# An encoder block on one core: the second blocks of its experts made small and interleaved, and its weight splits moved ahead

## The chip, the cores and the metric

The kernel runs on one core of a Trainium2 chip. The metric is the device time of one execution in microseconds (us), less is better. Engines are named as in the profile: PE is TensorE (matrix products), DVE is VectorE, ACT is ScalarE, POOL is GpSimd, and SP issues DMAs.

## The reference

The input is 2048 tokens of width 1024 in float32. The block normalises them, projects them, mixes them by windowed attention and by a bidirectional mLSTM, projects back and adds the residual. Then it sends each token to two of 32 experts:

```python
x = x + u @ w_out[l]
x = x + hier_moe(rmsnorm(x, norm2_g[l]), ...)        # top-1 group, then top-2 experts in it
...
return (jax.nn.silu(xb @ w_gate[e]) * (xb @ w_up[e])) @ w_down[e]     # 1024 -> 512 -> 1024
...
y = jnp.zeros((T, D), ys.dtype).at[row_tok].add(ys * row_w[:, None].astype(ys.dtype))
```

The routing of the reference's inputs gives 15 of the 32 experts more than 128 rows (130 to 180): experts 1, 7, 8, 10, 11, 14 to 17, 19, 20 and 27 to 30. None has more than 192.

## The kernel before

The first two thirds (projections, attention, mLSTM, merge, routing) are the same in both kernels. The change is in the last stage, the experts, which are run one after the other from 0 to 31.

Products are taken in split precision. A float32 matrix is written as a big half, rounded to the product's format, and a small half, the rest; a product is then three matrix products: big by big, small by big, big by small. For weights this is done on chip. An expert's weights come as six loads of 1 MB (`raw`, `rawd`; the SP queue issues them) and are cut into 12 pieces of 128x1024, eight of gate and up (`j` 0 to 7), four of down (8 to 11). `split` makes a piece: ACT copies the big half (`ehi`, L1560), and POOL for the pieces 1, 5, 8 and 10 (`POOL_J`), DVE for the others, subtracts the small half (`elo`, L1562). `wsplit(n)` splits piece n of all experts in a row (expert e begins at 12 e), and when both pieces of a load are split it issues the load six further on.

```python
    def wsplit(n):
        ...
        wts[n] = split(raws[n // 2], n % NPC)
        if n % 2:
            del raws[n // 2]
            wload(n // 2 + NRAW)
```

A block is up to 128 rows of an expert. POOL gathers its rows (`xg`; `xgB` for the second block) by an indirect DMA, PE transposes them (`xturn`, L1589), ACT and DVE split them into `xhi` and `xlo`. Then `Block.head` takes 48 products of 512 columns for gate and up (two halves `h` of the expert's width by eight row blocks by three), `act` makes `ha` (ACT's silu L1627, DVE's multiplication L1628), `turn` transposes it (PE L1634) and splits it (ACT L1635, DVE L1636), and 24 products follow for down, the last 12 in `Block.tail`. ACT and DVE scale half of the result each (`y`, L1703 and L1704), and POOL adds it to the output by an indirect DMA, a scatter (L1705). So a block is 72 products of 512 columns.

Each engine works through its own queue in the order of the program; semaphores order the queues against each other. The order is written by hand (`manual_schedule`): `between(i)` is called at five places of `head`, and the table `SPLITS` says which pieces are split at which place. When an expert begins, pieces 0 and 1 are split; 2 to 7 are split at the start of `head`, the rest in it. A second block runs within `tc.If(v > 1)` after the first, with its own 72 products over the same split weights, and nothing is split beside it.

Of the kernel before, what the change touches and what calls it, by code (L numbers as in the profile page):

```python
# [20 lines left out]
P = 128  # L21
# [19 lines left out]
def bucket_table():  # L41
    """Relative position to bucket, as one-hot rows, and the window's mask as a last row."""
# [12 lines left out]
class Chains:  # L55
    """Queues of generators, each advanced a step at a time between blocks of matrix products."""
# [55 lines left out]
def _body(tc, nc, A, out, scr_ext, upto, es):  # L112
# [68 lines left out]
    # gates of the mLSTM, all tokens: [i|f] x tile x (dir, head)  # L181
# [19 lines left out]
    PW = 272  # L201

    class Stream:
# [9 lines left out]
        def dma(self, n):  # L213
            """load half n % 2 of piece n // 2"""
# [70 lines left out]
    # order of the column pieces in a chunk of tokens  # L285
# [30 lines left out]
    def run_mms(mms, nsub=6):  # L316
        """mms: list of (out, lhsT, rhs, start, stop); chains advance between sub-blocks."""
# [11 lines left out]
    # ================= first half: projections, attention, forward mLSTM =================  # L329
# [19 lines left out]
    def small_loads():  # L349
# [7 lines left out]
        # per-channel vectors: conv taps (5), conv bias, merge biases, all halved  # L357
# [6 lines left out]
    def setup():  # L364
        """attention bias [query, head, key], per-channel columns, empty slots"""
# [26 lines left out]
        # a row of zeros past the tokens, weight 0  # L392
# [21 lines left out]
    # ---- rms norm and transposition of a tile of x  # L414
# [33 lines left out]
    # ---- attention  # L448
# [197 lines left out]
    def mload(t, d):  # L646
        """a tile's q and v; forward its k, backward what the forward pass left: k by rows and k q"""
# [15 lines left out]
    def mhead(n, t, d):  # L663
        """what a tile of the recurrence does without the state, at most a tile ahead of it"""
# [48 lines left out]
    def mtile(n, t, d):  # L713
        """one tile of the recurrence"""
# [71 lines left out]
    def mpost(n, t, h_):  # L786
        """both directions joined, normed and gated"""
# [32 lines left out]
    # ---- convolution over time, silu  # L820
# [17 lines left out]
    def conv_tail():  # L838
        """the last two tokens, with zeros behind them"""
# [77 lines left out]
    def qkv_done(c):  # L917
        """forward tiles of the mLSTM once a chunk's q, k and v are there"""
# [27 lines left out]
    # ---- projections  # L946
# [115 lines left out]
    # ================= second half: backward mLSTM, merge, output projection, routing =================  # L1062
# [12 lines left out]
    # the first tiles of these kinds, for the order of the kinds in memory  # L1075
# [7 lines left out]
    def after(t):  # L1083
        """makes what fills a tile wait for the first gated products"""
        nc.gpsimd.tensor_copy(t, uhi[:, 0, 0:1].bitcast(F32))
# [47 lines left out]
    def yprep_first(c):  # L1133
        """the same for the first chunk, in memory that holds the products later"""
# [41 lines left out]
    def bank(c, u):  # L1176
        """where the routing of a tile keeps its products"""
# [3 lines left out]
    def norm2(c, u):  # L1181
        """the residual and its norm go out; router logits of the tile, short of the norm's factor"""
# [44 lines left out]
    def table():  # L1227
        """rows and weights of the first two blocks of every expert, from the chunks before the last"""
# [367 lines left out]
    class Block:  # L1596
# [41 lines left out]
        def down_hi(self, k, h):  # L1638
            if k == 0:
                if h == 0:  # L1640
                    self.dn = []
# [155 lines left out]
```

## Time and profile before

| what | value |
|---|---|
| time, median of 3 runs (lowest to highest) | 2780.01 us (2776.28 to 2781.15) |
| profiled execution, first to last instruction | 2774.9 us |
| PE busy, of that span | 2562.3 us (92%) |
| DVE, ACT, POOL busy | 1556.6, 1283.7, 1243.0 us |
| experts' stage, 1786.6 to 2763.7 | 977.1 us, PE busy 888.2 |

Only the span of the profiled execution is given; the median of the runs lies 5.1 us above it. That PE is busy for 92% does not tell that it works at its pace: products are pipelined, and the time of one in a row is longer than the distance from one to the next.

### The profile page before, as it was taken

To read this page: it belongs to the slowest core of one execution; us is meant where nothing else is said; L and a number is where in the kernel's file an instruction comes from. 1 tells how busy PE (TensorE), PEld (TensorE's weight loads), DVE (VectorE), ACT (ScalarE), POOL (GpSimd) and SP (SyncE) were. 2 spreads that over 40 slices of the span, in tenths; PEclk is the share of its full clock that TensorE was granted. 3 is DMA by queue.
4 is the path that set the end of the run, shared out by engine and by line. 5 is a ranking of instruction groups with operands and counts; after the bars stand their busy time and mean duration, and the time that the engine had idled before them with its cause. 6 is when DMAs were issued, how large, how long until landed. Compare 5 with 4: busy or idle time off the path is not lost. (4 is left out here: it accounts for less than half of the span.)

```text
span 2774.9 us, 39144 instructions
## 1 busy us (share of the span) xinstructions
PE 2562.3 (92%) x14112; PEld 2129.0 (77%) x14113; DVE 1556.6 (56%) x2537; ACT 1283.7 (46%) x2500; POOL 1243.0 (45%) x1029
## 2 busy tenths in 40 slices
PE   7999999999999999978998989799999999988997
PEld 6778977897789787757977878677777777766775
DVE  4454445454545645558594937667454544567544
ACT  4444545454445444433332422357553544556543
POOL 5444444244433442324444445357643543545433
PEclk9999999999999999989999999899999999999998
DMA  5534434453345345477765644679876876779763
GB/s 159 156 113 149 135 111 121 141 160 107 114 137 161 114 127 164 148 195 213 230 199 179 186 152 127 223 252 344 283 257 191 297 242 195 266 232 324 267 194 109
DMA packets 348967, 518.68 MB, mean 187 GB/s; under 512 B 24747, under 2 KB 212228, under 8 KB 348748
## 3 DMA queue, kind: packets, MB, share of 16 engines
q1 hardware_dynamic: 332140, 460.03, 50.9%
q0 software_dynamic: 15440, 51.60, 7.9%
q10 hardware_dynamic: 1168, 4.21, 0.4%
q8 instruction: 126, 2.06, 0.3%
q14 instruction: 93, 0.76, 0.1%
HBM read 420.30 MB, written 95.47 MB: 186 GB/s over the span
## 5 line engine op out<-in xcount | busy, mean ns | idle before, releaser
L239 POOL TENSOR_TENSOR wlo<-wraw,whi 128x512 fp32r<-128x512 f32 (+1 forms) x422 | 572.7, 1386 | 472.4 <-ACT whi L236 454.4
L1618 PE MATMUL mm<-elo,xhi 128*128 128x512 f32 x752 | 276.2, 419 | 87.1 <-DVE elo L1562 50.5
L1562 DVE TENSOR_TENSOR elo<-raw,ehi 128x1024 fp32r<-128x1024 f32 x192 | 297.2, 1589 | 39.8 <-ACT ehi L1560 36.0
L1615 PE MATMUL mm<-ehi,xhi 128*128 128x512 f32 x752 | 307.6, 409 | 0.0
L319 PE MATMUL mm<-hThi,whi 128*128 128x512 f32 x768 | 306.9, 400 | 0.0
L319 PE MATMUL mm<-hTlo,whi 128*128 128x512 f32 x768 | 304.4, 396 | 0.0
L319 PE MATMUL mm<-hThi,wlo 128*128 128x512 f32 x768 | 304.0, 396 | 0.0
L1615 PE MATMUL mm<-ehi,xlo 128*128 128x512 f32 x752 | 302.4, 402 | 1.3 <-issue 1.3
L236 ACT ACTIVATE whi<-wraw 128x512 fp32r<-128x512 f32 (+1 forms) x424 | 233.4, 622 | 136.9 <-PE mm L319 59.1
L319 PE MATMUL mm<-whi,hThi 128*128 128x256 f32 (+1 forms) x896 | 260.3, 291 | 3.9 <-ACT ev L898 1.8
L319 PE MATMUL mm<-wlo,hThi 128*128 128x256 f32 (+1 forms) x896 | 256.0, 286 | 1.1 <-POOL wlo L239 1.1
L319 PE MATMUL mm<-whi,hTlo 128*128 128x256 f32 (+1 forms) x896 | 255.8, 285 | 0.0
L1618 PEld LDWEIGHTS mm<-elo,xhi 128*128 128x128 f32 x752 | 146.9, 198 | 139.8 <-DVE elo L1562 64.3
L1560 ACT ACTIVATE ehi<-raw 128x1024 fp32r<-128x1024 f32 x256 | 253.0, 1048 | 1.7 <-issue 0.5
L1705 POOL DMA_INDIRECT out<-y,idx x47 | 102.3, 2176 | 263.4 <-ACT ehi L1560 237.9
L1562 POOL TENSOR_TENSOR elo<-raw,ehi 128x1024 fp32r<-128x1024 f32 x64 | 156.4, 2444 | 127.9 <-ACT ehi L1560 127.2
L1562 POOL TENSOR_TENSOR elo<-rawd,ehi 128x1024 fp32r<-128x1024 f32 x64 | 163.9, 2560 | 79.0 <-ACT ehi L1560 79.0
L319 PEld LDWEIGHTS mm<-whi,hThi 128*128 128x128 f32 x896 | 170.2, 190 | 7.9 <-ACT ev L898 2.1
L319 PEld LDWEIGHTS mm<-wlo,hThi 128*128 128x128 f32 x896 | 170.3, 190 | 3.6 <-issue 1.6
L1615 PEld LDWEIGHTS mm<-ehi,xlo 128*128 128x128 f32 x752 | 147.5, 196 | 30.5 <-DVE xlo L1591 0.4
L319 PEld LDWEIGHTS mm<-hThi,wlo 128*128 128x128 f32 x768 | 144.3, 188 | 34.0 <-issue 3.2
L319 PEld LDWEIGHTS mm<-whi,hTlo 128*128 128x128 f32 x896 | 170.0, 190 | 0.3 <-DVE hTlo L444 0.2
(421 smaller groups left out, 5872.6 us busy)
## 6 DMA issues: line engine op xcount, KB each, us to landing
wraw<-w_in SPq DMA_DIRECT2D x152, 512.0 KB
raw<-w_expert_gate SPq DMA_DIRECT2D x128, 512.0 KB
raw<-w_expert_up SPq DMA_DIRECT2D x128, 512.0 KB
rawd<-w_expert_down SPq DMA_DIRECT2D x64, 1024.0 KB
mg_s<-evg SPq DMA_DIRECT2D x64, 256.0 KB
gt<-mg_s SPq DMA_DIRECT2D x32, 512.0 KB
wraw<-w_out SPq DMA_DIRECT2D x32, 512.0 KB
xt<-x SPq DMA_DIRECT2D x16, 512.0 KB
```

The lines of the kernel that those rows point to most:

```text
L236: nc.scalar.activation(hi[:, ks, :W], r[:, k:k + 2, :W], AF.Copy)
L239: eng.tensor_sub(lo[:, ks, :W], r[:, k:k + 2, :W], hi[:, ks, :W].bitcast(F32))
L319: nc.tensor.matmul(o, l, r, start=st, stop=sp)
L1560: nc.scalar.activation(dst[0], src, AF.Copy)
L1562: eng.tensor_tensor(dst[1], src, dst[0].bitcast(F32), op=OP.subtract)
L1615: nc.tensor.matmul(self.gu[h], x_[:, k, :], self.wt(k)[0][:, h, :], start=k == 0 and i == 0, stop=False)
L1618: nc.tensor.matmul(self.gu[h], self.xs[0][:, k, :], self.wt(k)[1][:, h, :], start=False, stop=stop)
L1705: nc.gpsimd.indirect_dma_start(out=out, out_offset=bass.IndirectOffsetOnAxis(ap=self.idx, axis=0), in_=y, in_offset=None, compute_op=OP.add)
```

## The change

A second block now has at most 64 rows. Its rows' big and small halves stand side by side in the 128 columns of one operand, so that the product with a weight's big half and that with its small half give all four partial products, in two passes and not three: 32 products for gate and up, 16 for down (`Small`). The two sets of 64 result rows are added at the end: for gate and up by eight products with a stacked identity (`fold`), for down by ACT and DVE. Its gate and up products stand after `middle` of the first block, its folds and down products beside and behind the first block's last ones. An expert with more than 192 rows takes its further blocks in the loop at the end, one block at a time.

The splits are moved. Of the next expert, pieces 2, 3 and 4 are split within the first block (after its gate and up products); pieces 5 to 13 are split in one run after the expert's last product. (`nxt` is the next expert's first piece; 12 and 13 belong to the one after it.) At the start all 14 pieces that there is room for are split.

```diff
--- before.py
+++ after.py
...
+    nc.vector.tensor_scalar(nbf, cnt[0:1, :], 192.0, None, op0=OP.is_gt)
+    nc.vector.scalar_tensor_tensor(nbf, cnt[0:1, :], 127.0, nbf, op0=OP.add, op1=OP.mult)
...
+        def begin(self):
+            for k in range(0, 4, 2):
+                for h in range(2):
+                    self.up(h, k, k + 2)
+            self.up(0, 4, KT)
             self.act(0)
+            self.room()
+        def middle(self):
             self.up(1, 4, 7)
             self.turn(0)
+            self.up(1, 7, KT)
+        def after(self, between=lambda i: None):
             self.act(1)
+            between(0)
+            self.down(0, (0, 1))
+            self.down(1, (0, 1))
+            between(1)
+            self.room()
             self.turn(1)
+            between(2)
+        def end(self, between=lambda i: None):
             between(0)
+            self.down(0, (2, 3))
             between(1)
+            self.down(1, (2, 3))
+            between(2)
             y = self.y
             nc.scalar.activation(y[:, 0:512], self.dn[0], AF.Copy, scale=self.wgt)
             nc.vector.tensor_scalar(y[:, 512:], self.dn[1], self.wgt, None, op0=OP.mult)
             nc.gpsimd.indirect_dma_start(out=out, out_offset=bass.IndirectOffsetOnAxis(ap=self.idx, axis=0),
                                          in_=y, in_offset=None, compute_op=OP.add)
...
+    class Small:
...
+        def turn(self):
+            for k in range(KT):
+                nc.tensor.transpose(self.p[:, k, :], self.xg[0:64, k * P:(k + 1) * P], ident[0:64, 0:64])
+            nc.scalar.activation(self.xs[:, :, 0, :], self.p, AF.Copy)
+            nc.vector.tensor_sub(self.xs[:, :, 1, :], self.p, self.xs[:, :, 0, :].bitcast(F32))
+        def product(self, ps, lhs, w, h, n):
+            for k in range(n):
+                for m in range(2):
+                    nc.tensor.matmul(ps, lhs[:, k].rearrange("p a t -> p (a t)"), w(k)[m][:, h, :],
+                                     start=k == 0 and m == 0, stop=k == n - 1 and m == 1)
+        def up(self):
+            for h in range(2):
+                self.product(self.ps[h], self.xs, self.wt, h, KT)
+        def copy(self):
+            nc.scalar.activation(self.g[:, 0, :], self.ps[0], AF.Copy)
+            nc.vector.tensor_copy(self.g[:, 1, :], self.ps[1])
+        def fold(self, h):
+            p = self.p[:, 4 * h:4 * h + 4]
+            for k in range(4):
+                nc.tensor.matmul(p[:, k, :], self.g[:, h, k * P:(k + 1) * P], sel, start=True, stop=True)
+            a = self.a[:, h]
+            nc.scalar.activation(a, p[:, 0:2], AF.Silu)
+            nc.vector.tensor_mul(a, a, p[:, 2:4])
+            hs = self.hs[:, 2 * h:2 * h + 2]
+            nc.scalar.activation(hs[:, :, 0, :], a, AF.Copy)
+            nc.vector.tensor_sub(hs[:, :, 1, :], a, hs[:, :, 0, :].bitcast(F32))
+        def down(self):
+            y = self.g[0:64].rearrange("p h f -> p (h f)")
+            ps = self.ps
+            for h in range(2):
+                self.product(ps[h], self.hs, lambda k: self.wt(8 + k), h, 4)
+                cs = slice(512 * h, 512 * h + 512)
+                nc.scalar.activation(y[:, cs], ps[h][64:128, :], AF.Copy)
+                nc.vector.tensor_add(y[:, cs], ps[h][0:64, :], y[:, cs])
+            nc.gpsimd.tensor_scalar(y, y, self.wgt[0:64, :], None, op0=OP.mult)
+            nc.gpsimd.indirect_dma_start(out=out, out_offset=bass.IndirectOffsetOnAxis(ap=self.idx[0:64, :], axis=0),
+                                         in_=y, in_offset=None, compute_op=OP.add)
-    SPLITS = {0: (2, 3, 4, 5, 6, 7), 1: (8,), 2: (9, 10), 3: (11,), 4: (12,)}
...
-    for n in range(RING - NPC):
+    two = mo.tile([1, 32], I32, name="two")
+    twof = mo.tile([1, 2, 32], F32, name="twof")
+    for i, n in enumerate((float(P), float(P + 64))):
+        nc.vector.tensor_scalar(twof[:, i], cnt[0:1, :], n, None, op0=OP.is_gt)
+    nc.vector.tensor_sub(two, twof[:, 0], twof[:, 1])
+    sel = mo.tile([P, 64], F32, name="sel")
+    for o in (0, 64):
+        nc.vector.tensor_copy(sel[o:o + 64, :], ident[o:o + 64, o:o + 64])
+    for n in range(6):
         wsplit(n)
     xsA = xtiles("")
     for i in range(2):
         xturn(xg[0], xsA, i, "")
+    for n in range(6, RING):
+        wsplit(n)
     for e in range(N_EXP):
-        v = nc.values_load(nb[:, e:e + 1], min_val=0, max_val=S // P)
-        nxt = {}
+        v = nc.values_load(two[:, e:e + 1], min_val=0, max_val=1)
+        nxt = NPC * (e + 1)
+        w_e = lambda k, e=e: wts[NPC * e + k]
         xgB = mo.tile([P, D], F32, name="xgB")
-        with tc.If(v > 1):
-            nc.gpsimd.indirect_dma_start(out=xgB, out_offset=None, in_=h2_ap,
-                                         in_offset=bass.IndirectOffsetOnAxis(ap=idx[:, 32 + e:33 + e], axis=0))
+        with tc.If(v > 0):
+            nc.gpsimd.indirect_dma_start(out=xgB[0:64, :], out_offset=None, in_=h2_ap,
+                                         in_offset=bass.IndirectOffsetOnAxis(ap=idx[0:64, 32 + e:33 + e], axis=0))
+        if e + 2 < N_EXP:
+            xg[e + 2] = gather(idx[:, e + 2:e + 3], "")
+        A_ = Block(w_e, xsA, idx[:, e:e + 1], wgt[:, e:e + 1])
+        B_ = Small(w_e, xgB, idx[:, 32 + e:33 + e], wgt[:, 32 + e:33 + e])
+        A_.begin()
+        with tc.If(v > 0) as cmp:
+            B_.turn()
+            A_.middle()
+            B_.up()
+        with cmp.Else():
+            A_.middle()
         def between(i):
-            if i == 0 and e + 2 < N_EXP:
-                xg[e + 2] = gather(idx[:, e + 2:e + 3], "")
-            if i == 4 and held:
+            if i == 0:
+                wsplit(nxt + 2)
+                wsplit(nxt + 3)
+            if i == 1 and held:
                 put(*held.pop(0))
-            for j in SPLITS.get(i, ()):
-                wsplit(NPC * e + j)
-            if i == 4 and e + 1 < N_EXP:
-                nxt["x"] = xtiles("")
-                for h in range(2):
-                    xturn(xg[e + 1], nxt["x"], h, "")
-                wsplit(NPC * e + 13)
-        A_ = Block(lambda k: wts[NPC * e + k], xsA, idx[:, e:e + 1], wgt[:, e:e + 1], "")
-        A_.head(between)
-        xsA = nxt.get("x")
-        with tc.If(v > 1) as cmp:
-            xsB = xtiles("B")
-            A_.tail(lambda i: xturn(xgB, xsB, i, "B"))
-            B_ = Block(lambda k: wts[NPC * e + k], xsB, idx[:, 32 + e:33 + e], wgt[:, 32 + e:33 + e], "B", xgB)
-            B_.head()
-            B_.tail()
+            if i == 2:
+                wsplit(nxt + 4)
+                if e + 1 < N_EXP:
+                    xs = xtiles("")
+                    for h in range(2):
+                        xturn(xg[e + 1], xs, h, "")
+                    return xs
+        nx = {}
+        def after(i):
+            nx["x"] = between(i)
+        A_.after(after)
+        with tc.If(v > 0) as cmp:
+            B_.copy()
+            def beside(i):
+                if i in (1, 2):
+                    B_.fold(i - 1)
+            A_.end(beside)
+            B_.down()
         with cmp.Else():
-            A_.tail()
-    # further blocks of experts with many rows
+            A_.end()
+        xsA = nx.get("x")
+        for n in range(5, RING):
+            wsplit(nxt + n)
     v = nc.values_load(most, min_val=0, max_val=S // P)
-    with tc.If(v > 2):
+    with tc.If(v > 1):
         with tc.For_i(0, N_EXP, 1) as e:
             v = nc.values_load(nb[:, bass.ds(e, 1)], min_val=0, max_val=S // P)
-            with tc.For_i(2, v, 1) as i:
+            with tc.For_i(1, v, 1) as i:
...
```

Three places show how the queues change. POOL, from one expert's scatters to the next expert's gathers (`out<-y` and `out<-g` are scatters, `xgB` and `xg` the gathers, the `TENSOR_TENSOR` rows subtract small halves); before:

```order
L1705 DMA out<-y,idx 2176x1024
L1745 ISA
L1745 UNCONDITIONAL_BRANCH
L1722 TENSOR_LOAD nb
L1725 COMPARE_AND_BRANCH
L1726 DMA xgB<-h_s,idx 128x1024
L1725 UNCONDITIONAL_BRANCH
L1725 ISA
L1725 UNCONDITIONAL_BRANCH
L1576 DMA xg<-h_s,idx 128x1024
L1562 TENSOR_TENSOR elo<-raw,ehi 128x1024
L1562 TENSOR_TENSOR elo<-rawd,ehi 128x1024 x2
```

The same place in the changed kernel:

```order
L1679 DMA out<-y,idx 2176x1024
L1802 ISA
L1802 UNCONDITIONAL_BRANCH
L1564 TENSOR_TENSOR elo<-raw,ehi 128x1024
L1564 TENSOR_TENSOR elo<-rawd,ehi 128x1024 x2
L1564 TENSOR_TENSOR elo<-raw,ehi 128x1024
L1762 TENSOR_LOAD two
L1766 COMPARE_AND_BRANCH
L1767 DMA xgB<-h_s,idx 64x1024
```

The gathers stood ahead of POOL's subtractions for an expert and now stand behind four of them.

DVE, from one expert's `y` to the next expert's first `ha`; before:

```order
L1704 TENSOR_SCALAR y<-mm,wgt 128x512
L1745 UNCONDITIONAL_BRANCH
L1722 TENSOR_LOAD nb
L1725 COMPARE_AND_BRANCH
L1725 UNCONDITIONAL_BRANCH x2
L1562 TENSOR_TENSOR elo<-raw,ehi 128x1024 x5
L1628 TENSOR_TENSOR ha<-ha,mm 128x256
```

and in the changed kernel:

```order
L1678 TENSOR_SCALAR y<-mm,wgt 128x512
L1802 UNCONDITIONAL_BRANCH
L1564 TENSOR_TENSOR elo<-raw,ehi 128x1024 x2
L1564 TENSOR_TENSOR elo<-rawd,ehi 128x1024 x2
L1564 TENSOR_TENSOR elo<-raw,ehi 128x1024
L1762 TENSOR_LOAD two
L1766 COMPARE_AND_BRANCH
L1766 UNCONDITIONAL_BRANCH x2
L1623 TENSOR_TENSOR ha<-ha,mm 128x256
```

Five subtractions stand ahead of `ha` in both; the five were the running expert's pieces 2, 3, 4, 6 and 7, and are now 6, 7, 9, 11 and the next expert's 0.

PE, where the second block's rows are transposed. Before, behind the first block's last transposes, three quarters through it:

```order
L1589 MATMUL tr<-ident,xg 128x128 x8
L1745 COMPARE_AND_BRANCH
L1589 MATMUL tr<-ident,xgB 128x128 x4
L1644 MATMUL mm<-ehi,hh 128x512
L1645 MATMUL mm<-elo,hh 128x512
```

and now, behind the first 36 products of an expert, ahead of the other 12 of gate and up:

```order
L1617 MATMUL mm<-elo,xhi 128x512
L1775 COMPARE_AND_BRANCH
L1696 MATMUL tr<-ident,xgB 128x64 x8
L1617 MATMUL mm<-ehi,xhi 128x512
L1617 MATMUL mm<-ehi,xlo 128x512
L1617 MATMUL mm<-elo,xhi 128x512
```

PE's need of `xgB` has moved from the last quarter of the first block's products to their middle.

## Rows read from the trace of the kernel before

**Rows 1.** Stretches (experts 23, 24, 16, all): length, busy, clock, DMA share, GB/s.

```profile
2488.70:2512.60 23.90, 19.75 (x86) 15.40 (x85) 18.27 (x15) 14.69 (x20) 13.18 (x7) 0.93 0.91 310
2512.60:2532.90 20.30, 18.65 (x85) 14.54 (x84) 15.90 (x15) 14.79 (x20) 14.63 (x7) 1.00 0.93 315
2259.70:2298.20 38.50, 36.32 (x170) 29.05 (x169) 17.26 (x22) 18.10 (x27) 16.53 (x8) 1.00 0.67 218
1786.60:2763.70 977.10, 888.22 (x3941) 702.61 (x3940) 551.03 (x584) 520.56 (x711) 486.59 (x226) 0.96 0.76 251
```

**Rows 2.** PE's waits in the experts' stage: us in total, times, longest.

```profile
PE mm L1618 <- DVE elo L1562: 50.5, 20, 4.2
PE mm L1618 <- POOL elo L1562: 36.1, 19, 2.2
```

**Rows 3.** Timeline of PE in expert 23: start, us, instruction [idle before].

```profile
2494.33 0.39 PE L1615 MATMUL mm<-ehi,xlo 128*128 128x512 f32 x1
...
2495.92 0.39 PE L1618 MATMUL mm<-elo,xhi 128*128 128x512 f32 x1
2500.45 1.93 PE L1618 MATMUL mm<-elo,xhi 128*128 128x512 f32 x3 [4.15 <-DVE elo L1562]
2502.18 0.63 PE L1615 MATMUL mm<-ehi,xhi 128*128 128x512 f32 x1
...
2503.87 0.40 PE L1615 MATMUL mm<-ehi,xlo 128*128 128x512 f32 x1
```

**Rows 4.** Timeline of ACT at the start of expert 23.

```profile
2488.54 0.69 ACT L1703 ACTIVATE y<-mm,wgt 128x512 f32<-128x512 f32 x1 [0.82 <-ACT ehi L1560]
2489.14 5.80 ACT L1560 ACTIVATE ehi<-raw 128x1024 fp32r<-128x1024 f32 x6
```

**Rows 5.** Timeline of POOL in the same expert.

```profile
2490.45 2.46 POOL L1705 DMA_INDIRECT out<-y,idx  x1 [0.26 <-ACT ehi L1560]
...
2494.64 2.38 POOL L1562 TENSOR_TENSOR elo<-raw,ehi 128x1024 fp32r<-128x1024 f32 x1
2496.97 2.34 POOL L1562 TENSOR_TENSOR elo<-rawd,ehi 128x1024 fp32r<-128x1024 f32 x1
```

**Rows 6.** Timeline of DVE in the same expert.

```profile
2488.92 0.75 DVE L1704 TENSOR_SCALAR y<-mm,wgt 128x512 f32<-128x512 f32 x1 [0.81 <-issue]
2490.24 3.50 DVE L1562 TENSOR_TENSOR elo<-raw,ehi 128x1024 fp32r<-128x1024 f32 x3 [0.56 <-ACT ehi L1560]
2494.03 7.51 DVE L1562 TENSOR_TENSOR elo<-raw,ehi 128x1024 fp32r<-128x1024 f32 x2 [0.29 <-ACT ehi L1560]
```

**Rows 7.** Timelines of POOL and DVE in expert 4, the same place.

```profile
1899.55 2.47 POOL L1562 TENSOR_TENSOR elo<-raw,ehi 128x1024 fp32r<-128x1024 f32 x1
1901.99 3.39 POOL L1562 TENSOR_TENSOR elo<-rawd,ehi 128x1024 fp32r<-128x1024 f32 x1
...
1898.51 4.60 DVE L1562 TENSOR_TENSOR elo<-raw,ehi 128x1024 fp32r<-128x1024 f32 x2 [0.29 <-ACT ehi L1560]
```

**Rows 8.** The gathers by tile, xgB and then xg: from issue to landing.

```profile
DMA to landing us min/median/max: 8.2/8.4/9.8
...
DMA to landing us min/median/max: 5.3/8.4/10.2
```

**Rows 9.** Groups of the stage by form: busy us, mean ns, idle before.

```profile
L1628 DVE TENSOR_TENSOR ha<-ha,mm 128x256 f32<-128x256 f32 x94 | 39.6, 422 | 202.5 <-ACT ha L1627 202.5
L1590 ACT ACTIVATE xhi<-tr 128x512 fp32r<-128x512 f32 x94 | 52.5, 598 | 12.4 <-PE tr L1589 10.6
```

**Rows 10.** Timeline of PE: small products in routing, the first transposes, later ones.

```profile
1758.21 1.08 PE L1392 MATMUL mm<-fe,fh 128*128 128x64 f32 x8
...
1784.84 1.97 PE L1589 MATMUL tr<-ident,xg 128*128 128x128 f32 x8 [5.97 <-DMA xg<-h_s,idx]
...
2276.32 1.19 PE L1589 MATMUL tr<-ident,xg 128*128 128x128 f32 x8
2277.35 0.60 PE L1589 MATMUL tr<-ident,xgB 128*128 128x128 f32 x4
```

More of the change, by code (lines that the diff above doesn't have):

```diff
@@ L1604, in __init__ @@
                                   for i in range(2))
-            self.y = mo.tile([P, D], F32, name="y", tag="y" + tag)
-            self.gu = [self.ps(h) for h in range(2)]
-        def ps(self, h):
-            if self.tag:
-                return mp.tile([P, 512], F32, name="mm", tag=f"a{h}" + self.tag)
-            return mp.tile([P, 512], F32, name="mm", tag="a", bufs=3)
-        def up_x(self, h, k):
-            for i, x_ in enumerate(self.xs):
-                nc.tensor.matmul(self.gu[h], x_[:, k, :], self.wt(k)[0][:, h, :], start=k == 0 and i == 0, stop=False)
@@ L1617, in up_w, with ps @@
-        def up_w(self, h, k, stop=False):
-            nc.tensor.matmul(self.gu[h], self.xs[0][:, k, :], self.wt(k)[1][:, h, :], start=False, stop=stop)
+            self.y = mo.tile([P, D], F32, name="y")
+            self.gu = [self.ps() for h in range(2)]
+            self.dn = []
+        def ps(self):
+            return mp.tile([P, 512], F32, name="mm", tag="a", bufs=3)
         def up(self, h, k0, k1):
             for k in range(k0, k1):
-                self.up_x(h, k)
-                self.up_w(h, k, k == KT - 1)
+                hi, lo = self.wt(k)
+                for m, (x_, w_) in enumerate(((self.xs[0], hi), (self.xs[1], hi), (self.xs[0], lo))):
+                    nc.tensor.matmul(self.gu[h], x_[:, k, :], w_[:, h, :], start=k == 0 and m == 0,
+                                     stop=k == KT - 1 and m == 2)
@@ L1632, in turn @@
-            p = mp.tile([P, 4, P], F32, name="tr", tag="tr" + self.tag, bufs=1 if self.tag else 2)
+            a, hhi, hlo, p = self.a, self.hhi, self.hlo, self.p
             for k in range(2):
@@ L1672, in head @@
+        def begin(self):
[3 more added lines that the diff above has]
+            self.up(0, 4, KT)
             self.act(0)
-            between(2)
+            self.room()
+        def middle(self):
             self.up(1, 4, 7)
             self.turn(0)
-            self.up(1, 7, 8)
+            self.up(1, 7, KT)
+        def after(self, between=lambda i: None):
             self.act(1)
-            between(3)
-            for k in range(2):
-                self.down_hi(k, 0)
@@ L1681, in head @@
-            if self.tag:
-                for k in range(2):
-                    self.down_lo(k, 0)
-            for k in range(2):
-                self.down_hi(k, 1)
-            self.turn(1)
-            for h in range(1 if self.tag else 0, 2):
-                for k in range(2):
-                    self.down_lo(k, h)
-            between(4)
-        def tail(self, between=lambda i: None):
+            between(0)
+            self.down(0, (0, 1))
+            self.down(1, (0, 1))
+            between(1)
@@ L1772, in _body @@
                         wt[n] = split(r, n)
-                G = Block(wt.get, xs, ix, en[:, 1:2], "")
-                G.head()
-                G.tail()
+                G = Block(wt.get, xs, ix, en[:, 1:2])
+                G.begin()
+                G.middle()
+                G.after()
+                G.end()
 _INS = ["x", "norm1_g", "w_in", "attn_q_gain", "attn_k_gain", "attn_sink", "rel_bias_table",
```

70 lines of the change are left out of this document (24 added, 46 removed).

## The prediction

> **What bounds the kernel now.** Only the experts' stage differs between the two kernels, so I read it first, by stretch [rows 1]: 977.1 us of the 2774.9, PE busy for 888.2. An expert without a second block takes 20.3 us (24) or 23.9 (23), one with a second block 38.5 (16). Then PE's waits there [rows 2]: all but a few are for small halves of weights, 50.5 us for DVE's and 36.1 for POOL's. The timeline of PE shows one of them [rows 3]: products stand 0.227 us apart (seven steps from 2494.33 to 2495.92), then PE waits 4.15 us, and after it seven steps take 3.42 us (2500.45 to 2503.87) and not 1.6: the granted clock is at the lower of its two levels, 1.2 and not 2.4 GHz, which costs 1.8 more. The mean clock of that expert is 0.93; of the next, without so long a wait, 1.00 [rows 1].
>
> Why DVE is late stands in three timelines of expert 23, whose first product is at 2488.70; I call that moment T. ACT makes big halves 0.95 apart (six in 5.80) [rows 4]. POOL begins its scatter at T+1.75 and has 2.46 to do, then a gather, then two subtractions of 2.4 [rows 5]; the scatter needs DVE's half of `y`, which ends at T+1.0 [rows 6]. DVE subtracts in 1.17 (three in 3.50), but the pair at 2494.03 takes 7.51 [rows 6]: the first of it ends only when POOL's two are over (2499.31). In expert 4 a DVE subtraction that came during POOL's first got its turn behind it, and POOL's second took 3.39 for 2.34, waiting in turn [rows 7]. So POOL and DVE never subtract at the same time; mostly they alternate, and one of them can be passed over. The Trainium skill (SBUF — State Buffer, "Who interferes with whom") has it as a lock: a DVE instruction with two inputs in SBUF and a POOL instruction that reads SBUF exclude each other, the first to start holding it throughout. The exclusion agrees with 7.51; the order does not always, since the DVE row of 2494.03 had started 0.6 us ahead of POOL's and lost to two. Both orders are summed below.
>
> **What the change does, and its prices.**
>
> *PE's work.* A second block has 48 products in place of 72 (24 x 0.227 = 5.4 us less). Its row transposes shrink and its four of `ha` go: 12 at 0.13 before (eight from 2276.32 to 2277.35), 8 of half the columns at about 0.07 now, 1.0 less. Eight folds come: eight products of that output form took 1.08 [rows 10]. Net 5.3 us, times 15 = 80 us less of PE's work. That is a gain only if nothing is late.
>
> *The splits, an expert behind one without a second block.* The order of the queues tells what stands behind what; times are from T, its first product. ACT's half of `y` began at T-0.16 and the first big half 0.6 later [rows 4]; its last product now stands four products earlier (0.9), so the nine big halves start at -0.5: piece 5 is there at +0.6, 9 at +4.4, 12 at +7.2, 13 at +8.2. POOL's scatter holds it to +4.2 as before. DVE ends its `y` at +1.0 and pieces 6 and 7 by +4.0. From there the two alternate: POOL piece 5 until 6.7, DVE 9 until 7.8, POOL 8 until 10.1, DVE 11 until 11.2, POOL 10 until 13.5, DVE 12 until 14.6, POOL 13 until 16.9.
>
> Queued behind DVE's piece 12 is `ha` (0.42 [rows 9]): it is ready at +15.0. PE has 36 products of `begin` (8.2) and nine more, is at +10.2 when it needs `ha`, and waits 4.8. Then: 27 products 6.1, 12 transposes 1.6, the low clock 1.8, and about 0.4 for a PSUM buffer of the next transposes, which `turn(1)`'s small half behind two splits on DVE frees late: 9.9, so 24.9 for the expert. Behind one with a second block POOL has a scaling and a second scatter first; between nothing and one subtraction (2.4) each, I take 1 us in all: 25.9.
>
> *The gather, an expert with a second block.* Its gather stands behind POOL's piece 13: issue at +17.2. It landed 8.2 to 9.8 us after issue before, other gathers 5.3 to 10.2 [rows 8]. With half the rows I take 7.5, between the fastest and the median: +24.7. PE wants these rows right behind `begin`, at +8.2, and everything else of both blocks is queued behind them: it waits 16.5 us. Then 8 transposes 0.6, 84 products 19.1, 12 transposes 1.6, folds 1.1, the low clock 1.8, and 1.6 for the end, where two `xhi` copies (0.6 each [rows 9]) and a split stand ahead of the copy that the fold needs: 25.8. So 50.5 us, and 51.5 behind another second block, against 38.5 before.
>
> *The rest.* The weights' loads: 310 to 315 GB/s ran in experts of 20 to 24 us [rows 1]; the new experts are longer, so no load is late. The four splits that now stand ahead of the first transposes (3.8 us of ACT) lie within PE's 5.97 wait for the first gather [rows 10], and would cost up to 3.8 without it, as the few new small instructions would. Branches cost PE nothing that the rows show, there being no idle before its products but for weights [rows 2]. The loop is not entered, no expert having over 192 rows.
>
> *Sum.* Expert 0 has all pieces under way early, so it lies between no wait (72 products, 12 transposes and the low clock, 19.7) and 24.9: 21. Expert 31 turns no next rows: 24.5. Ten experts (3 to 6, 13, 22 to 26) at 24.9 = 249, five (2, 9, 12, 18, 21) at 25.9 = 130, six with a second block behind one without (1, 7, 10, 14, 19, 27) at 50.5 = 303, nine behind another at 51.5 = 464. Together 1191, against 977: 214 us more. The profiled execution's span would go from 2774.9 to 2989, and the median, 5.1 us above that span before, to **2994**.
>
> If POOL always goes first: its four end at 4.2 + 4 x 2.35 = +13.6, DVE's three at 17.1, so `ha` is at 17.5 and an expert without a second block takes 27.4; the gather lands at +21.4 and one with takes 47.2 (a us more each behind a second block). The sum is about 1180, a median of 2983: nearly the same, one loss for the other. The order in which the two engines take turns hardly matters.
>
> **The rivals.**
>
> *The gather lands sooner.* The fastest seen is 5.3. With POOL first that is +19.2, experts of 45.0 and 46.0: 15 x 2.2 less than that, 2950; landing 3 us after issue, as nothing here shows, would give 2983 - 15 x 4.5 = 2916. The Trainium skill (DMA: Bandwidth & Descriptors, "Anatomy of one DMA") fits a POOL-issued DMA by 2.0 us and its bytes over 436 GB/s, 2.6 us for these 256 KB; an estimate by that page is 2994 - 15 x 4.9 = 2920. The rows speak against it: 8.4 in the median for 512 KB [rows 8].
>
> *Faster.* One mechanism could turn the sign: the gather not held up by the burst. Without the first block's and the gather's waits an expert takes 17.9 (72 products and 12 transposes) and one with a second block 30.5: 17 x 17.9 + 15 x 30.5 = 762, a median of 2565. What decides is when the rows land. With experts of 24.9, an expert with a second block must stay under 37, a landing before +11; with DVE always first (`ha` at 12.8, experts of 22.7) under 39.2, before +13.4. But piece 13's big half is there at +8.3 only, its subtraction takes 2.4, and the fastest landing 5.3: +16 even if POOL had nothing else. For it speaks only that PE's work falls by 80 us and that the old waits (87 us) would go.
>
> *No change.* The same with a landing at +11 to +13.4; or the second blocks' saving just paying for the waits. The rows leave no room for it.
>
> *Slower still.* Landing at 10.2, the slowest seen, adds 2.7 x 15 = 40: 3034; if the low clock costs twice as much after 16 us of idling as after 4, 15 x 1.8 = 27 more: 3061.
>
> **How the numbers follow.** A measurement here can tell about 0.2% (5.6 us) from no change. The forecast, between 2960 and 3045 with its bounds, has 0.74; the gather sooner (2890 to 2960) 0.13; slower still 0.07; faster 0.04; no change 0.02. So slower 0.94. The range of 8 in 10 is 2905 to 3050.
>
> **What would show it.** Right: PE's largest wait is for `xgB`, 15 times some 16 us, and its second for `ha` at L1623, some 16 times near 5; the gather's issue on POOL 17 us after an expert's first product; granted clock about 0.9; experts of 25 and 50 us. Wrong: PE waiting for `elo` as before, or gathers issued ahead of POOL's subtractions, or experts with a second block under 40 us.

## The result and the profile after

The changed kernel took 3038.85 us in the median (3036.52 to 3045.31), the kernel before 2778.58 on the same chip: a ratio of 1.0947, interval 1.0929 to 1.0965. That is slower by 260 us, 45 us above the forecast of 2994 and within its range. The profiled execution's span is 3036.0 us.

The stretches of the changed kernel answer to [rows 1]: experts 6 and 7 (behind an expert without a second block), 8 (behind one with), and the stage; columns as there.

```profile
1968.00:1995.30 27.30, 20.03 (x85) 15.75 (x84) 22.15 (x15) 14.57 (x20) 15.67 (x7) 0.87 0.82 257
1995.30:2044.40 49.10, 35.25 (x157) 27.89 (x156) 25.79 (x23) 17.02 (x26) 18.05 (x9) 0.86 0.53 172
2044.40:2096.50 52.10, 36.13 (x158) 28.33 (x157) 25.46 (x23) 18.02 (x27) 18.04 (x10) 0.84 0.52 151
1785.20:3025.30 1240.10, 884.49 (x3762) 693.59 (x3760) 751.53 (x595) 513.14 (x722) 522.11 (x242) 0.85 0.61 192
```

The stage grew by 263 us. PE is busy for 884.5 us of it, hardly less than the 888.2 before, though it has 360 products fewer: at the lower clock each takes longer. PE's waits (us in total, times, longest) against [rows 2]:

```profile
PE tr L1696 <- DMA xgB<-h_s,idx: 193.2, 15, 14.3
PE tr L1631 <- DVE ha L1623: 93.7, 17, 6.8
PE mm L1617 <- POOL elo L1564: 44.1, 15, 3.7
PE tr L1591 <- DVE hh L1633: 18.5, 31, 0.7
```

The old waits for DVE's small halves are gone, and the first two lines are those forecast. The third, 15 times, is for POOL's small halves, now in experts behind a second block alone. Timeline of POOL in expert 7 (first product at 1995.3, which is T), then in expert 8 (T at 2044.4), against [rows 5]:

```profile
1997.09 2.47 POOL L1679 DMA_INDIRECT out<-y,idx  x1 [11.16 <-POOLq L1802]
1998.99 3.01 POOL L1564 TENSOR_TENSOR elo<-raw,ehi 128x1024 fp32r<-128x1024 f32 x1
2001.45 5.18 POOL L1564 TENSOR_TENSOR elo<-rawd,ehi 128x1024 fp32r<-128x1024 f32 x2
2006.11 2.82 POOL L1564 TENSOR_TENSOR elo<-raw,ehi 128x1024 fp32r<-128x1024 f32 x1
2009.09 1.75 POOL L1767 DMA_INDIRECT xgB<-h_s,idx  x1 [0.16 <-issue]
...
2046.12 2.85 POOL L1734 TENSOR_SCALAR g<-g,wgt 64x1024 f32<-64x1024 f32 x1 [1.59 <-DVE g L1733]
2049.96 1.50 POOL L1735 DMA_INDIRECT out<-g,idx  x1 [0.98 <-POOL g L1734]
2050.98 2.87 POOL L1564 TENSOR_TENSOR elo<-raw,ehi 128x1024 fp32r<-128x1024 f32 x1
```

In expert 7 POOL subtracts four pieces without a break, and issues the gather at T+13.8. In expert 8 its first piece is over at 2053.85, T+9.4, for T+6.7 in expert 7: the second block's scaling and scatter stand ahead of it. DVE in expert 7, against [rows 6]:

```profile
1996.86 2.36 DVE L1564 TENSOR_TENSOR elo<-raw,ehi 128x1024 fp32r<-128x1024 f32 x2 [0.54 <-ACT ehi L1562]
1999.70 11.45 DVE L1564 TENSOR_TENSOR elo<-rawd,ehi 128x1024 fp32r<-128x1024 f32 x2 [0.47 <-ACT ehi L1562]
2011.08 1.21 DVE L1564 TENSOR_TENSOR elo<-raw,ehi 128x1024 fp32r<-128x1024 f32 x1
2012.21 0.41 DVE L1623 TENSOR_TENSOR ha<-ha,mm 128x256 f32<-128x256 f32 x1
```

Two subtractions of 1.2 each take 11.45: the first of them, begun during POOL's first, is then passed over by POOL's other three. `ha`, queued behind, is there at T+17.3. PE, against [rows 3], and the gather's landing, against [rows 8]:

```profile
2003.57 0.39 PE L1617 MATMUL mm<-elo,xhi 128*128 128x512 f32 x1
2016.74 1.09 PE L1696 MATMUL tr<-ident,xgB 64*128 64x64 f32 x8 [12.78 <-DMA xgB<-h_s,idx]
...
2018.35 0.63 PE L1617 MATMUL mm<-ehi,xlo 128*128 128x512 f32 x1
...
2021.33 0.63 PE L1617 MATMUL mm<-elo,xhi 128*128 128x512 f32 x1
...
2022.95 0.39 PE L1617 MATMUL mm<-elo,xhi 128*128 128x512 f32 x1
```

```profile
DMA to landing us min/median/max: 7.3/8.1/9.3
```

PE waits 12.78 us for the rows, and the seven steps from 2018.35 to 2021.33 are 0.426 apart, the lower level of the clock; it is back by 2022.95, 6.2 us after the wait.

### The profile page after: what moved, and what is told of

The parts are those of the page before. It is cut to its first block, busy times and chain, and to the rows that moved or that the text cites. A ratio compares the mean times of both kernels' runs of the same rounds, so it can differ in the third digit from the quotient of the medians.

```text
span 3036.0 us, 39208 instructions
## 1 busy us (share of the span) xinstructions
PE 2565.5 (85%) x13932; PEld 2127.1 (70%) x13933; DVE 1761.2 (58%) x2558; ACT 1278.8 (42%) x2515; POOL 1278.6 (42%) x1044
## 5 line engine op out<-in xcount | busy, mean ns | idle before, releaser
L1564 DVE TENSOR_TENSOR elo<-rawd,ehi 128x1024 fp32r<-128x1024 f32 x64 | 356.0, 5582 | 25.7 <-ACT ehi L1562 25.7
L1679 POOL DMA_INDIRECT out<-y,idx x32 | 64.1, 2002 | 666.8 <-issue 457.3
L1564 DVE TENSOR_TENSOR elo<-raw,ehi 128x1024 fp32r<-128x1024 f32 x192 | 234.8, 1252 | 56.6 <-ACT ehi L1562 56.6
L1617 PE MATMUL mm<-elo,xhi 128*128 128x512 f32 x512 | 225.5, 440 | 44.1 <-POOL elo L1564 44.1
L1617 PE MATMUL mm<-ehi,xhi 128*128 128x512 f32 x512 | 228.5, 446 | 0.0
L1617 PE MATMUL mm<-ehi,xlo 128*128 128x512 f32 x512 | 221.8, 433 | 0.0
L1643 PE MATMUL mm<-ehi,hh 128*128 128x512 f32 x512 | 189.8, 429 | 0.6 <-ACT hh L1632 0.6
L1564 POOL TENSOR_TENSOR elo<-raw,ehi 128x1024 fp32r<-128x1024 f32 x64 | 183.3, 2865 | 0.5 <-ACT ehi L1562 0.5
L1696 PE MATMUL tr<-ident,xgB 64*128 64x64 f32 x120 | 16.3, 315 | 193.2 <-DMA xgB<-h_s,idx 193.2
```

The costliest lines, as they stand in the source:

```text
L1564: eng.tensor_tensor(dst[1], src, dst[0].bitcast(F32), op=OP.subtract)
L1617: nc.tensor.matmul(self.gu[h], x_[:, k, :], w_[:, h, :], start=k == 0 and m == 0, stop=k == KT - 1 and m == 2)
L1643: nc.tensor.matmul(self.dn[h], h_[:, k, :], w_[:, h, :], start=k == 0 and m == 0, stop=k == 3 and m == 2)
L1679: nc.gpsimd.indirect_dma_start(out=out, out_offset=bass.IndirectOffsetOnAxis(ap=self.idx, axis=0), in_=y, in_offset=None, compute_op=OP.add)
L1696: nc.tensor.transpose(self.p[:, k, :], self.xg[0:64, k * P:(k + 1) * P], ident[0:64, 0:64])
```

## The experiments

The theory: PE waits because POOL's four and DVE's last three subtractions of the run exclude each other, and behind them stand `ha` and the gather; the small form itself saves PE's work. The rivals: the small form costs what it saves, or one engine or queue alone is at fault. All kernels, and the mean time of an expert (from its first product to the next one's, from the traces; A is without, B with a second block, B/A is B behind A). Each ratio is to runs of the kernel before on the same chip, whose median was 2771 to 2779 us:

| kernel | median us | ratio to before | stage | A/A | A/B | B/A | B/B |
|---|---|---|---|---|---|---|---|
| before | 2778.6 | | 977 | 21.9 | 24.4 | 38.5 | 40.0 |
| changed | 3038.9 | 1.0947 | 1240 | 27.2 | 30.0 | 48.8 | 52.8 |
| e1_gather_ahead | 2896.9 | 1.0451 (1.0422 to 1.0480) | 1105 | 27.5 | 29.7 | 41.0 | 42.8 |
| e2_dve_only | 2787.0 | 1.0061 (1.0039 to 1.0083) | 997 | 20.4 | 22.4 | 40.1 | 44.2 |
| e3_before_dve_only | 2677.5 | 0.9668 (0.9646 to 0.9690) | 884 | 19.1 | 18.6 | 38.1 | 37.1 |
| e4_small_alone | 2785.4 | 1.0053 (1.0021 to 1.0084) | 977 | 22.5 | 22.9 | 38.3 | 40.6 |
| e5_both | 2691.6 | 0.9723 (0.9698 to 0.9749) | 901 | 20.7 | 23.2 | 33.9 | 36.9 |
| e6_keep_small | 2838.3 | 1.0256 (1.0227 to 1.0285) | 1041 | 22.2 | 26.4 | 41.6 | 43.4 |
| e7_keep_small_dve | 2795.8 | 1.0093 (1.0060 to 1.0126) | 1006 | 19.9 | 21.7 | 41.2 | 45.4 |
| e8_scale_dve | 3023.2 | 1.0913 (1.0886 to 1.0939) | 1228 | 27.4 | 29.5 | 48.5 | 51.7 |
| e9_small_alone_dve | 2706.0 | 0.9757 (0.9739 to 0.9774) | 913 | 18.7 | 19.7 | 39.1 | 39.3 |
| e10_keep_ahead_dve | 2688.5 | 0.9701 (0.9683 to 0.9720) | 893 | 19.9 | 21.4 | 35.4 | 36.9 |
| e11_piece5_dve | 2970.0 | 1.0709 (1.0691 to 1.0726) | 1175 | 25.1 | 28.0 | 48.4 | 49.7 |
| e12_small_covered | 2648.8 | 0.9532 (0.9512 to 0.9552) | 843 | 18.8 | 19.5 | 34.8 | 34.5 |

**e1_gather_ahead: the changed kernel, with the next expert's `xgB` gathered behind `middle`, ahead of the run of splits.**

```diff
-        xgB = mo.tile([P, D], F32, name="xgB")
-        with tc.If(v > 0):
-            nc.gpsimd.indirect_dma_start(out=xgB[0:64, :], out_offset=None, in_=h2_ap,
+        xgB = xgBs.pop(e)
...
             A_.middle()
+        if e + 1 < N_EXP:
+            xgBs[e + 1] = gatherB(e + 1)
```

> The changed kernel with one thing moved: the gather of the next expert's second block is issued behind the middle of the running expert, so ahead of the run of nine splits. Theory (the 193 us that PE waits for xgB are the gather standing behind POOL's four subtractions): that wait goes to nothing; in its place these experts wait for ha until about T+17.5, as the others do, so one with a second block takes about 41 us behind one without and 45 behind another, in place of 49 and 53: 115 to 120 us less, 2920 us. Rival (the second block is late for another reason, its splits or folds, and the gather merely ends last): the time stays within 20 us of 3039.

2896.9, 142 us less, for 115 to 120 expected. PE's waits:

```profile
PE tr L1631 <- DVE ha L1623: 160.9, 32, 7.0
PE mm L1617 <- POOL elo L1564: 36.9, 15, 3.7
```

None is for `xgB`. Now every expert waits for `ha`, up to 7.0 us, and A/A stays at 27.5.

**e2_dve_only and e3_before_dve_only: all subtractions on DVE, in the changed kernel and in the one before.**

```diff
-    POOL_J = (1, 5, 8, 10)
+    POOL_J = ()
```

> The changed kernel with all subtractions of the experts' weights on DVE (POOL_J empty), so POOL has only gathers and scatters and the two never exclude each other. Theory: DVE does nine splits 1.14 apart, ha is ready near T+11.8, the gather is issued right behind the scatters, near T+4.7 (behind a second block near T+7.5) and lands 7.6 to 8.2 later, so experts take about 21, 38 and 41.5 us and the median is about 2760 (2730 to 2800). Rival (DVE alone is too slow for twelve pieces an expert, and the splits are the bound): experts of 25 us and more without a second block, 2900 or above.

> The kernel before with the same edit (POOL_J empty), the control for the run with all subtractions on DVE. Theory: the waits of 87 us for small halves came of POOL and DVE excluding each other, so most of them and of the low clock behind them go: experts of 18.7 to 19.5 us without a second block, 36.3 to 37 with, a median of 2670 to 2710. Rival (POOL took work that DVE has no time for): 2780 or more, PE waiting for elo of DVE alone.

2787.0 and 2677.5. In the changed kernel (first fence) the gather now goes right behind the scatters, and still lands after PE wants it (expert 7: T+12.9 for +8.5); the waits for `ha` are down to 2.8 and less. There DVE does all nine subtractions ahead of `ha`, and not five, and yet `ha` is there at T+11.6 and not +17.3: so POOL held it up, and not a lack of time on DVE. In the kernel before (second fence) 11.7 us of waits for small halves are left of 86.6, and it is 3.3% faster by this one number.

```profile
PE tr L1696 <- DMA xgB<-h_s,idx: 106.0, 15, 8.9
PE tr L1631 <- DVE ha L1623: 25.9, 17, 2.8
```

```profile
PE mm L1618 <- DVE elo L1562: 11.7, 29, 0.4
PE mm L1644 <- ACT hh L1635: 5.4, 4, 2.1
```

**e5_both: e1 and e2 together.**

> The changed kernel with both edits: the second block's gather ahead of the run of splits, and all subtractions on DVE. Theory: the two waits have separate causes and both edits keep their worth; experts without a second block stay at 20.4 and 22.1 us, those with one fall from 40 and 44 to about 33 and 35.5, the rest being ha behind nine splits on DVE: 2680 (2650 to 2710). Rival (the gather's wait covered other late work, folds or loads): 2740 or more.

2691.6: 347 us less than the changed kernel, and 2.8% less than before. The two single gains (142 and 252) add up to more, since DVE alone also lets the gather go earlier: in e2 the waits for `xgB` had fallen from 193.2 to 106.0. No wait for `xgB` is left, and of those for `ha`:

```profile
PE tr L1631 <- DVE ha L1623: 42.8, 28, 2.8
```

The 2.8% are not a gain of the change: the kernel before with the same number (e3) is 3.3% faster. With both waits dealt with, the change as it is placed here still gains nothing on that.

**e4_small_alone: the kernel before, with its second blocks in the small form, behind the first block.**

```diff
-            xsB = xtiles("B")
-            A_.tail(lambda i: xturn(xgB, xsB, i, "B"))
-            B_.head()
-            B_.tail()
+            B_.turn()
+            B_.up()
+            B_.copy()
+            A_.tail(lambda i: B_.fold(0) if i == 1 else None)
+            B_.fold(1)
+            B_.down()
```

> The kernel before, with its own order of splits, and only the second blocks made small (64 rows, two passes, folds beside the first block's tail), so the split part of the change is left out. PE's work should fall by about 5 us for each of 15, less some 2 us of waits in the fold chain: 3 x 15 = 45 us less if nothing else is late, about 2735. Against it: the scaling on POOL (2.85 us in the changed kernel) and the second scatter stand ahead of POOL's subtraction of piece 5 of the next expert, which PE waits for already: up to 3.5 us and the low clock, 1.8, for each of 14 next experts, 74 us, so 2780 to 2810. I take 2775.

2785.4 (2768.6 to 2802.1), no gain. In the profiled run, one of the faster with 2770.1, the waits for POOL are twice those of [rows 2], and one for the transposed rows is new:

```profile
PE mm L1618 <- POOL elo L1562: 71.5, 26, 3.7
PE mm L1729 <- DVE xs L1724: 33.5, 15, 2.3
PE mm L1618 <- DVE elo L1562: 25.0, 11, 4.1
```

**e6_keep_small: the changed kernel with its splits put back to where they stood before. e7_keep_small_dve: the same, on DVE alone.**

```diff
+        for j in range(2, 9):
+            wsplit(NPC * e + j)
         A_.begin()
+        for j in (9, 10):
+            wsplit(NPC * e + j)
...
-                wsplit(nxt + 2)
-                wsplit(nxt + 3)
+                wsplit(NPC * e + 11)
...
-        for n in range(5, RING):
-            wsplit(nxt + n)
```

> The changed kernel with the split part undone: pieces 2 to 13 of an expert are split at the places of the kernel before, two pieces ahead, POOL keeping its four; the small second blocks stay as they are, beside the first block's products, and the gathers stand ahead of POOL's subtractions again. Theory (the loss is all of the split part): the waits for xgB go, experts without a second block are those of the kernel before, 22 us and some 2 to 4 more behind a second block for POOL's scaling; with one 34 to 39: 2720 to 2770, faster than before by 10 to 60 us. Rival (the small blocks themselves, their folds and branches, cost what they save): 2780 or more.

> The same with all subtractions on DVE: the kernel before with DVE alone took 2677.5 with experts of 18.6 and 37.1 us. Theory (two passes save 5.3 us of PE's work for each of 15 blocks, and nothing else is late): 18.6 and about 32 to 32.5, so 70 to 75 us less, 2605 (2590 to 2630). Rival (weights' loads become the bound as experts get shorter, 6.3 MB and the gathers at 310 to 370 GB/s being 20 us an expert): waits for ehi appear in the runs of experts without a second block, 2640 or more.

Both missed: 2838.3 and 2795.8. So the moved splits are not alone at fault. In e6 the waits for `xgB` are down to 2.9 us in all: POOL's run no longer stands ahead of it, and PE comes to it later, since it waits for POOL's pieces (first fence). In e7 PE comes to `xgB` sooner than it lands (second); e7's rival, the loads, fell too, as PE has no wait for `ehi`.

```profile
PE mm L1617 <- POOL elo L1564: 94.1, 37, 4.8
PE mm L1617 <- DVE elo L1564: 17.7, 31, 2.2
```

```profile
PE tr L1696 <- DMA xgB<-h_s,idx: 87.9, 15, 8.3
```

Why POOL is waited for more in e6 than before was not tried. The order of the products may be part of it: `head` took the small halves in the order 4, 6, 5, 7, `begin` takes POOL's piece 5 in its turn.

**e10_keep_ahead_dve: e7 with the gather of e1.**

> e7 (the small blocks inside the first block, the splits where they were before, DVE alone subtracts) with the one edit that the next expert's xgB is gathered behind the first block's middle instead of at the expert's start. Theory (e7's loss was xgB alone, 87.9 us of PE's waits and the low clock behind them): 2795.8 less 88 and some 15 to 30 us of low clock, 2680 us, between 2650 and 2710; no waits for xgB. Rival (the splits in the middle also cost, as the waits for hh and fold in e7 showed, or PE is late for another piece once xgB is there): 2730 or above.

2688.5, 107 us less than e7 and as expected, with no wait for `xgB`. That is the larger part of the 191 us by which e7 missed 2605, and not all: the other 83 are in every kind of expert. e7 was to have 18.6 without a second block and 32 to 32.5 with one; here B/A is at 35.4 and B/B at 36.9, and A/A at 19.9 where e3 has 18.5 to 18.6 in most. Two waits for `hh` of 0.5 each are part of that; the rest was not tried.

**e8_scale_dve and e11_piece5_dve: the changed kernel with the second block's scaling on DVE; with piece 5 on DVE.**

```diff
-            nc.gpsimd.tensor_scalar(y, y, self.wgt[0:64, :], None, op0=OP.mult)
+            nc.vector.tensor_scalar(y, y, self.wgt[0:64, :], None, op0=OP.mult)
```

```diff
-    POOL_J = (1, 5, 8, 10)
+    POOL_J = (1, 8, 10)
```

> The changed kernel with the scaling of the second block's result on DVE in place of POOL. It tests the term taken as 1 us for what POOL has more to do behind a second block. Theory (2.85 us of scaling and a second scatter of 1.5 push POOL's piece 5 beyond the moment at which PE needs it, and the next gather too): without the scaling the 44 us of PE's waits for POOL's elo fall below 10, the experts behind a second block get 3 to 5 us shorter, 15 x 4 = 60 less, 2980. Rival (the waits come of the second scatter or of the lock alone): less than 20 us, 3020 or more.

> The changed kernel with one number changed: piece 5 is subtracted on DVE, so POOL keeps three pieces (1, 8, 10). Theory (behind a second block PE waits because POOL's first piece of the run stands behind the second scatter, 44 us of waits; ha and xgB are late by the number of POOL's subtractions ahead of them, 2.4 to 2.9 us each): the waits for elo go, ha comes 1 to 2.5 us earlier (17 times 1 to 2.5 us less of 93.7 us), xgB about 2 us earlier (15 x 2), and some low clock with them: 2920 us, between 2880 and 2960. Rival (POOL begins the run late for whatever piece it has first, and DVE is held just as long): 2990 or above, with the waits for elo now on piece 8.

3023.2 for e8: a miss, on the rival's side. The waits for POOL's `elo` are still 36.3 us. POOL's scatter in expert 8 of e8 (T at 2045.9), with DVE's rows:

```profile
2047.43 0.75 DVE L1734 TENSOR_SCALAR g<-g,wgt 64x1024 f32<-64x1024 f32 x1
2048.61 2.36 DVE L1564 TENSOR_TENSOR elo<-raw,ehi 128x1024 fp32r<-128x1024 f32 x2 [0.44 <-ACT ehi L1562]
...
2051.30 1.43 POOL L1735 DMA_INDIRECT out<-g,idx  x1 [5.32 <-DVE elo L1564]
```

The scaling takes 0.75 and not 2.85, yet the scatter begins at T+5.4, for 5.6 in the changed kernel: it comes behind DVE's two subtractions, 3.1 us after what it needs is there. Why it is held so long was not settled.

2970.0 for e11: 69 us less, of 119 expected. The waits for `elo` are gone, and `ha` is there at T+14.7 in A/A. But `xgB` is no earlier behind an A, T+21.1 for 21.4: with three pieces POOL and DVE take turns there (behind a B, POOL goes first). POOL in expert 7 of e11 (T at 1987.1):

```profile
1990.56 6.49 POOL L1564 TENSOR_TENSOR elo<-rawd,ehi 128x1024 fp32r<-128x1024 f32 x2
1997.01 3.31 POOL L1564 TENSOR_TENSOR elo<-raw,ehi 128x1024 fp32r<-128x1024 f32 x1
2000.48 1.75 POOL L1767 DMA_INDIRECT xgB<-h_s,idx  x1 [0.15 <-issue]
```

Three subtractions in turns take 9.8 us, nearly as long as four in a row in the changed kernel, and the gather goes at T+13.4.

**e9_small_alone_dve: e4 with all subtractions on DVE.**

> The kernel before with only its second blocks made small, still behind the first block (as in e4), and with all the subtractions on DVE (as in e3). Theory (the two passes do save PE's work, some 5 us for a second block, and what ate it in e4 were the waits of POOL's subtractions, 71.5 us there): from 2677.5 us (e3) 15 x 5.3 = 80 us come off and 15 x 2.6 us of waits for the transposed rows and for hs go on, 2640 us, between 2615 and 2660; no waits for POOL, waits for xs about 33 us. Rival (the small form costs as much as it saves, whoever subtracts): 2677 or above.

2706.0: a miss, on the rival's side, 28 us above e3. Its expert 10, PE:

```profile
2047.86 0.71 PE L1722 MATMUL tr<-ident,xgB 64*128 64x64 f32 x8
2051.74 0.79 PE L1729 MATMUL mm<-ehi,xs 128*128 128x512 f32 x1 [3.17 <-DVE xs L1724]
2052.33 0.63 PE L1729 MATMUL mm<-elo,xs 128*128 128x512 f32 x1
...
2056.60 0.63 PE L1729 MATMUL mm<-elo,xs 128*128 128x512 f32 x1
2057.03 0.48 PE L1729 MATMUL mm<-ehi,xs 128*128 128x512 f32 x1
```

PE waits 3.17 us for the rows' halves, which stand on ACT and DVE behind the next block's and one piece's, and then has eleven steps in 4.70 us (2052.33 to 2057.03), 2.2 more than at 0.227. That is the 5 us that the small form was to save.

**e12_small_covered: e9 with the small block's waits covered by products of PE.**

```diff
             B_.turn()
-            B_.up()
-            B_.copy()
-            A_.tail(lambda i: B_.fold(0) if i == 1 else None)
-            B_.fold(1)
-            B_.down()
+            A_.tail()
+            B_.upfold()
+            B_.down()
```

`upfold` makes the products of half 0, then those of half 1 with `fold(0)` in their middle; `down` now has `fold(1)` behind its first four products, of half 0.

> e9 (the kernel before, small second blocks behind the first, all subtractions on DVE) with the small block's waits covered: the first block's last 12 products stand between its transposes and its first product, the first fold stands between its gate and up products, and the second between its down products. Nothing else differs, and PE's work is the same. Theory (the two passes do save some 5 us of PE's time for a second block, and e9 gave that back in the wait for xs, 50.5 us in all, and in the low clock behind it, 0.912 to 0.956 in these experts): xs is waited for 0.3 to 0.6 us and the clock stays at 1.00, 4 to 5 us off each of 15 experts: 2635 us, between 2615 and 2660. Rival (the small form saves nothing at any place): 2690 or above.

2648.8: the theory held. PE's waits, and the stretch of its expert 14:

```profile
PE mm L1618 <- DVE elo L1562: 21.1, 46, 0.7
PE mm L1729 <- DVE xs L1724: 6.5, 15, 2.3
```

```profile
2131.60:2165.20 33.60, 32.61 (x158) 25.64 (x158) 20.90 (x28) 18.22 (x27) 7.44 (x4) 1.00 0.95 336
```

The clock is at 1.00. It is the fastest kernel of the study, 4.7% below the kernel before. Of it, 3.3% are e3's one number.

## Why the prediction was right, and which terms were off

*The mechanism.* Right. Both forecast waits are PE's first two; e1 takes away the one, e2 most of the other (93.7 to 25.9 us), and e5 the first and much of the second (42.8, for 160.9 in e1). One sign of being wrong came too, in part: PE still waits for POOL's `elo`.

*The order of POOL and DVE.* The forecast's sum took turns. Behind an expert without a second block the trace has POOL first fifteen times, and turns once. For POOL first the prediction had `ha` at T+17.5, and PE goes on at +17.5; the expert 27.4, measured 27.3 for expert 6; the gather's issue and landing +13.6 and +21.4, measured +13.8 and, by PE's first transpose, +21.4. Against the sum in turns that is 2.3 us more in ten A/A (+23 us) and 1.75 less in six B/A (-10). The turns came in expert 3 (T at 1889.0):

```profile
1893.64 6.22 DVE L1564 TENSOR_TENSOR elo<-rawd,ehi 128x1024 fp32r<-128x1024 f32 x2 [0.48 <-ACT ehi L1562]
1903.06 0.41 DVE L1623 TENSOR_TENSOR ha<-ha,mm 128x256 f32<-128x256 f32 x1
1895.39 6.67 POOL L1564 TENSOR_TENSOR elo<-rawd,ehi 128x1024 fp32r<-128x1024 f32 x2
```

There `ha` is ready at +14.5 and the expert takes 24.5, for the forecast +15.0 and 24.9. So each sum holds for its own order; what decides between the orders was not settled. The Trainium skill (SBUF — State Buffer, "Who interferes with whom") gives the lock to whichever starts first. The exclusion agrees with all these rows; that order agrees with expert 3, but not with expert 7, where DVE's row at 1999.70 had started 1.75 us ahead of POOL's second.

*Behind a second block: the term that was mis-sized most.* Taken as 1 us between nothing and 2.4 each for the scaling and the scatter. Measured by the table, A/B less A/A is 2.8 and B/B less B/A 4.0, so it is short by 9 us over the five A/B and by 27 over the nine B/B. POOL's first piece is over 2.5 to 3.8 later than behind an A, and with it come later `ha` in the A/B and the gather, issued at T+16.3 to 17.6, in the B/B. PE also waits for that piece (44.1 us), which the forecast did not have; but it is the run behind it that counts: e11, which has no such wait, still has A/B 2.9 above A/A, while B/B less B/A falls to 1.3 with the gather at T+14.7.

*The gather's landing.* Taken as 7.5, measured 8.1 in the median, 7.3 to 9.3, for 64 rows; 8.4 for 128 before [rows 8]. In the B/A it was 7.3 to 7.6, in the B/B 7.9 to 9.3, which is a part of the 4.0 above. The rival of a sooner landing fell: the estimate by the Trainium skill (DMA: Bandwidth & Descriptors, "Anatomy of one DMA"), 2.6 us, is a third of it.

*The remaining 25.8 us of an expert with a second block.* Measured 26.6 to 28.0 in the B/A; the stage's mean clock was 0.85, for about 0.9 forecast. The cost of the low clock was taken from the wait of 4.15 us, as 1.8. Behind the wait of 12.78 it is back only by 2022.95, 6.2 us after PE goes on, for 3.4 in [rows 3]; set against the full clock's distances, those rows give a loss of nearly 3, an estimate. The folds are the other part (next paragraph).

*PE's work.* Taken as 5.3 us less for a second block, 80 us in all. The stage in e3 (first fence) and in e12, both with a mean clock of 1.00, has PE busy for:

```profile
1777.10:2661.40 884.30, 860.70 (x3941) 681.23 (x3940) 601.45 (x710) 519.42 (x711) 183.37 (x99) 1.00 0.81 278
```

```profile
1787.00:2630.20 843.20, 806.67 (x3761) 628.60 (x3760) 611.15 (x725) 523.08 (x726) 209.06 (x114) 1.00 0.82 287
```

That is 54 us less, 3.6 each and not 5.3. Of the missing 1.7 the folds are 1.0, by a misreading: in [rows 10] the eight rows of that output form, 1.08 us, are four products of the program, two rows each. The eight folds of a second block are 16 rows, in e12 31.6 us for 15 blocks, 2.1 each; the other 0.7 stays open.

```profile
L1744 PE MATMUL tr<-sel,g 128*128 128x64 f32 x240 | 31.6, 274 | 0.0
```

So in the changed kernel, where PE is busy for only 4 us less than before, some 50 us of the saving went to the lower clock.

*Sum.* By kind, measured less the forecast's sum in turns (A/B and B/B hold the order's part too): A/A +23, A/B +20, B/A -10, B/B +12, experts 0 and 31 +5: 49 us; 4 come off around the stage (it begins 1.4 earlier, and the median is 2.9 above the span, not 5.1). Expert 0 was taken as 21 and took 25.9: it waits 4.4 for `ha` as the others do. The prediction's own sum for POOL first, the order that came, is some 60 us short (1180 for 1240), 41 of them in the B/B: that the sum in turns comes nearer is luck, its B/A being too long.

*The rivals.* "Faster" asked for a gather that the run does not hold up. e1 shows that this is not enough (2896.9), and e2, where the exclusion is gone but the gather still late, is not faster either (2787.0); it takes both (e5). "Slower still" named 3034, near the time, but for a landing at 10.2; its other term, a dearer low clock, came in part.

## What to carry to other kernels

Ask of every run of work that is moved what stands behind it on each queue, a gather's issue above all, and add the two engines' times where they exclude each other; sharing work with an engine that locks the first out can be worse than leaving it all on one (e3). A saving of PE's work counts only if nothing opens up in front of its products: by the ratios to the kernel before, the same small blocks lost 0.9% behind a wait of 3.2 us (e9 against e3) and gained 1.4% with the wait covered (e12 against e3). Cover such waits by the order of the products before judging the form.

## What the runs showed of the hardware

- A DVE subtraction of two SBUF operands, 1.2 us by itself, took 10.3 us (11.45 for two) against a run of four on POOL, though it had begun ahead of three of them. POOL's own took 2.8 to 3.0. In expert 3 of the same run the two engines took turns (POOL 6.67 for two). Against a run of three (e11) they took turns behind an expert without a second block (POOL 6.49 for two) and did not behind one with.
- The clock: 11 products at the lower level behind 3.17 us of waiting in e9, 2.2 us lost; 1.39 us of waiting in e12's expert 7 left its mean at 1.00, 2.3 us in its expert 27 took it to 0.95.
- A gather of 64 rows lands hardly sooner than one of 128: 8.1 for 8.4 us in the median.
